# ScalarE and GpSimd in written order while the first half of the values is made

## The chip, the core and the metric

The kernel runs on one core of a Trainium2 chip. The metric is the device time of one execution in microseconds (us). A core has five engines that run at the same time, each with its own list of instructions: TensorE (PE) multiplies matrices into PSUM, VectorE (DVE), ScalarE (ACT) and GpSimd (POOL) work on elements, SyncE (SP) issues most DMA transfers. Each engine works through its list in order; an instruction whose input is not there holds up all that stand behind it on that engine.

## The reference

One inference step of a two-layer decoder on 512 prompt tokens with 16 meta tokens ahead, and on 8 sequences of 4 new tokens: 560 rows of 1024 in all. The first layer is RWKV-7 time mixing, the second latent attention; a squared-ReLU MLP follows each. What matters here is the start of the first layer:

```python
def rwkv7_time_mix(xn, prev, s0, p, i):
    xx = prev - xn
    mu = p['rw_mu'][i]
    xr, xw, xk, xv, xa, xg = (xn + xx * mu[m] for m in range(6))
    r = xr @ p['rw_wr'][i]
    k = xk @ p['rw_wk'][i]
    v = xv @ p['rw_wv'][i]
    w_log = -softplus(-(p['rw_w0'][i] + tanh(xw @ p['rw_w1'][i]) @ p['rw_w2'][i])) - 0.5
    a = sigmoid(p['rw_a0'][i] + (xa @ p['rw_a1'][i]) @ p['rw_a2'][i])
    g = sigmoid(xg @ p['rw_g1'][i]) @ p['rw_g2'][i]
    ...
```

Here xn is the normalised input and prev the row before it. The large products are r, k and v; those with w1, a1 and g1 are narrow (64, 64 and 128 columns) and are called low-rank products here.

## The kernel before, in words

Activations lie feature by feature: eight slices of 128 features (k = 0 to 7), each with the 560 rows as columns. For the values the columns are taken in two spans, 256 and 304. Large products are made three times over, from a rounded high part and a low part (the rest) of each operand: a weight block of 128 x 1024 is loaded by SyncE into one of two buffers `raw`, cast on ScalarE (`whi`), and its low part subtracted on VectorE (`wlo`); the activations are rounded on ScalarE and their low parts subtracted on VectorE in the same way.

`rwkv` makes the first half of the values in one block, `with tc.manual_schedule(engines=MS)` at L537. Within it the engines in the set MS keep the order in which the program is written; all other engines, and all engines outside of it, get their order from a list scheduler, which takes by its own estimate what is ready next. Before, MS holds VectorE alone.

The block first loads two weight blocks (`wload`, casts at L487). Then a loop of 18 steps runs a pipeline over 16 pieces (8 slices for the first span, then 8 for the second). In step n it does, in this written order:

- `s1` of piece n: normalise (L519, VectorE); the difference to the row before (L522, VectorE for some slices, GpSimd for the others); for the first span one column on ScalarE (L524), for the second span the starts of the eight sequences on GpSimd (L526) and a copy for an output on ScalarE (L527);
- in steps 1, 4, 6 and 8 `wlo_`: the low part of the next weight block (L493, VectorE). The first two of these then load and cast the third and the fourth block, which need the buffer that L493 has just read: DMA at L484, cast on ScalarE at L487;
- `s2` of piece n-1: the mix for the values (L447, VectorE) and its rounding `xvh` (L531, ScalarE);
- `s3` of piece n-2: the low part `xvl` (L535, VectorE), and TensorE's products (L503).

Behind the loop the block copies the values of the first span out of PSUM (L514, two on VectorE, two on ScalarE), prefetches the next weight block (cast L307 on ScalarE, low part L308 on VectorE), and makes the low-rank mixes of the eight slices: `lw` on VectorE (L447); two `lm` by `amix`, each a multiplication on ScalarE (L452) and an addition on GpSimd (L453), 15 of them (the last is on VectorE). The copies of the second span stand behind slice 0 of these.

Behind the block follow the low-rank products (L578, L579, L341), the tanh and sigmoid parts, the receptance and key mixes (L447, L459, L460), transposes of the values (`v_out`, L601 to L608), and `stage_a` (L677, L678) and `stage_r` (L326), with which the long part of the layer begins. A product of `stage_r` takes one of the two PSUM buffers that those of L677 hold until ScalarE has read them (L678).

Of the kernel before, what the change touches and what calls it, by code (L numbers as in the profile page):

```python
# [205 lines left out]
class Kern:  # L206
# [203 lines left out]
    def rwkv(self):  # L410
# [64 lines left out]
            nc.scalar.activation(rstd[:, s], q[:, :n], AF.Ln, scale=1.0 / D, bias=self.eps[:, 0:1])  # L475
            nc.scalar.activation(rstd[:, s], rstd[:, s], AF.Exp, scale=-0.5)
        held = lambda n: self.bq_.tile([128, 1024], F32R, tag="b", name=n, bufs=self.nb)
        MS = {mybir.EngineType.DVE}
        raws, wv = [], []

        def wload(*ii):
            for i in ii:
                raw = self.wp.tile([128, 1024], F32, tag="raw", name=f"raw{i}", bufs=2)
                nc.sync.dma_start(raw, self.I["wall"][self.wseq[i]])  # L484
                raws.append(raw)
                hi, lo = held("whi"), held("wlo")
                nc.scalar.copy(hi, raw)  # L487
                wv.append((hi, lo))
            self.wi += len(ii)
# [46 lines left out]

        with tc.manual_schedule(engines=MS):  # L537
            wload(0, 1)
# [1385 lines left out]
```

## Time and profile before

| | |
|---|---|
| median of 3 runs | 1707.78 us (1706.32 to 1708.18) |
| the profiled execution | 1705.09 us |
| its span, first to last instruction | 1703.3 us |
| TensorE busy | 1575.3 us (92%) |
| VectorE busy | 972.1 us (57%) |
| ScalarE busy | 667.0 us (39%) |
| GpSimd busy | 348.4 us (20%) |

The profile is one execution of the kernel, with all times in us from the span's start. A busy share is a mean over stages that are bound by different things. A row of the order in time gives start, duration and the instruction; in square brackets stands how long the engine was idle before it, and for whom it waited. An instruction's duration includes the time in which it has been issued but does not get on.

### The profile page before, as it was taken

The page shows a single profiled execution, that of the slowest core. Times are in us where ns is not written, and L with a number is a line of the kernel's source. Part 1 is how long each engine was busy: PE and PEld are TensorE (multiplying, and loading weights), DVE is VectorE, ACT ScalarE, POOL GpSimd, SP SyncE. Part 2 cuts the span into 40 slices and gives each one's busy share as a digit, 9 for nine tenths or more (in the row PEclk, how much of TensorE's full clock was granted, in tenths as well). Part 3 has the DMA queues.
Part 4 walks back from the last instruction along what each step waited for, and adds up shares of the span by engine and source line. Part 5 has one row for each costly group of instructions (what it writes and reads, how often), then busy time and mean ns, then how long its engine had stood idle before and what let it go on. Part 6 is the DMA issues. An engine that isn't in the chain of part 4 may idle for free.

```text
span 1703.3 us, 33334 instructions
## 1 busy us (share of the span) xinstructions
PE 1575.3 (92%) x13474; PEld 1442.5 (85%) x13474; DVE 972.1 (57%) x1601; ACT 667.0 (39%) x1236; POOL 348.4 (20%) x467
## 2 busy tenths in 40 slices
PE   7699897798899997999999999899999999999996
PEld 6478786686689886999999998767679999999996
DVE  6775678465466677555444656555635444444456
ACT  4374545333445443443331442344534331322222
POOL 3623525442111123000000012773500000000000
PEclk9889897698899998999999999999999999999998
DMA  6334556977834454454232243787612222222223
GB/s 206 128 94 129 181 148 189 256 219 191 241 117 156 158 184 140 137 156 129 87 100 78 86 145 117 230 284 222 190 51 81 91 90 87 88 87 87 87 88 102
DMA packets 156475, 240.04 MB, mean 141 GB/s; under 512 B 68417, under 2 KB 100082, under 8 KB 156322
## 3 DMA queue, kind: packets, MB, share of 16 engines
q1 hardware_dynamic: 140466, 189.59, 36.9%
q0 software_dynamic: 15280, 47.59, 8.5%
q8 instruction: 106, 1.74, 0.4%
q10 hardware_dynamic: 576, 0.74, 0.1%
q14 instruction: 47, 0.39, 0.1%
HBM read 200.50 MB, written 37.37 MB: 140 GB/s over the span
## 4 chain that ended last, share of the span: by engine, by line
PE 54%; DVE 2%; ACT 2%; DMA 1%; issue 1%; SPq 1%; POOL 0%; DVEq 0%; ACTq 0%; POOLq 0%
PE mm L326 31%; PE mm L337 12%; PE sm L337 2%; PE sm L1749 2%; PE sm L1656 1%; PE sm L1700 1%; ACT whi L307 1%; PE sm L1602 1%; DMA lN<-latN,idx 1%; PE sm L1640 0%; DVE wlo L308 0%; PE sm L1703 0%; DMA raw<-wall 0%; DVE y L1861 0%; PE mm L1616 0%
## 5 line engine op out<-in xcount | busy, mean ns | idle before, releaser
L307 ACT CAST whi<-raw 128x1024 fp32r<-128x1024 f32 x218 | 228.8, 1050 | 639.7 <-PE mm L326 356.9
L308 DVE TENSOR_TENSOR wlo<-raw,whi 128x1024 fp32r<-128x1024 f32 x214 | 267.4, 1250 | 280.1 <-ACT whi L307 278.2
L337 PE MATMUL mm<-xs,whi 128*128 128x256 f32 (+1 forms) x1024 | 201.0, 294 | 1.4 <-DVE fd L1316 0.9
L337 PEld LDWEIGHTS mm<-xs,whi 128*128 128x128 f32 x1024 | 163.9, 190 | 2.6 <-issue 1.4
L337 PE MATMUL mm<-xs,wlo 128*128 128x256 f32 (+1 forms) x512 | 149.9, 293 | 0.0
L326 PE MATMUL mm<-hh,wlo 128*128 128x272 f32 (+1 forms) x640 | 133.5, 290 | 0.0
L326 PE MATMUL mm<-hl,whi 128*128 128x272 f32 (+1 forms) x640 | 133.4, 290 | 0.0
L326 PE MATMUL mm<-hh,whi 128*128 128x272 f32 (+1 forms) x640 | 133.3, 290 | 0.0
L326 PE MATMUL mm<-h_ffn,whi 128*128 128x272 f32 x512 | 106.2, 289 | 0.5 <-ACT fr L1350 0.5
L326 PE MATMUL mm<-l_ffn,whi 128*128 128x272 f32 x512 | 105.8, 288 | 0.0
L326 PE MATMUL mm<-h_ffn,wlo 128*128 128x272 f32 x512 | 105.4, 287 | 0.0
L326 PEld LDWEIGHTS mm<-hh,whi 128*128 128x128 f32 x640 | 101.1, 188 | 0.0
L326 PEld LDWEIGHTS mm<-hh,wlo 128*128 128x128 f32 x640 | 100.9, 188 | 0.0
L326 PEld LDWEIGHTS mm<-hl,whi 128*128 128x128 f32 x640 | 100.7, 188 | 0.0
L337 PEld LDWEIGHTS mm<-xs,wlo 128*128 128x128 f32 x512 | 97.1, 190 | 0.1
L1859 POOL TENSOR_TENSOR y<-x,rstd 128x272 f32<-128x272 f32 x4 | 3.5, 895 | 456.6 <-DVE wlo L308 449.7
L337 PE MATMUL mm<-hh,wlo 128*128 128x256 f32 (+1 forms) x256 | 76.2, 298 | 5.0 <-DVE wlo L308 5.0
L326 PEld LDWEIGHTS mm<-h_ffn,whi 128*128 128x128 f32 x512 | 79.9, 188 | 1.0 <-ACT fr L1350 1.0
L326 PEld LDWEIGHTS mm<-l_ffn,whi 128*128 128x128 f32 x512 | 80.2, 188 | 0.0
L326 PEld LDWEIGHTS mm<-h_ffn,wlo 128*128 128x128 f32 x512 | 80.1, 188 | 0.0
L337 PE MATMUL mm<-hl,whi 128*128 128x256 f32 (+1 forms) x256 | 75.8, 296 | 3.0 <-DVE hl L1308 3.0
L337 PE MATMUL mm<-hh,whi 128*128 128x256 f32 (+1 forms) x256 | 76.5, 299 | 0.1
(472 smaller groups left out, 3824.3 us busy)
## 6 DMA issues: line engine op xcount, KB each, us to landing
raw<-wall SPq DMA_DIRECT2D x222, 512.0 KB, 3.6
lT<-latT SPq DMA_DIRECT2D x80, 160.0 KB, 3.6
W_D<-sc POOLq DMA_DIRECT2D x16, 512.0 KB, 3.8
W<-W_D SPq DMA_DIRECT2D x32, 256.0 KB, 4.7
AK_D<-akt SPq DMA_DIRECT2D x8, 576.0 KB, 4.6
s<-state SPq DMA_DIRECT2D x16, 256.0 KB, 3.2
AKc<-AK_D SPq DMA_DIRECT2D x16, 256.0 KB, 4.3
V_D<-vt POOLq DMA_DIRECT2D x8, 288.0 KB, 6.3
```

What stands on the lines that cost most here:

```text
L307: nc.scalar.copy(hi, raw)
L308: self.lo_on.tensor_sub(lo, raw, hi.bitcast(F32))
L326: nc.tensor.matmul(v[:, h, :], wt[:, k, :], xt[:, off + h * n: off + (h + 1) * n], start=(first and k == 0 and e == 0), stop=(last and k = ...
L337: self.nc.tensor.matmul(v, wt[:, k, :], xt, start=(k == 0 and e == 0), stop=(k == len(xs) - 1 and e == 2))
L1602: nc.tensor.matmul(o, l[:, k0:k0 + kw], w[:, 2 + k, :], start=(k == 0 and e == 0), stop=(k == 1 and e == 2))
L1656: nc.tensor.matmul(q[:, q0:], V[h // 2][b][:, 128 * (h % 2):128 * (h % 2) + 128], PT[b] if b else Pm[h % 2], start=(b == 0), stop=(b == 4))
L1700: nc.tensor.matmul(q[32 * bb:32 * bb + 32, cols], qlT[:, r, 4 * g + bb, :], lt[bb][:, :, 128 * r + 64 * k:128 * r + 64 * k + 64], start=(r ...
L1749: nc.tensor.matmul(qa[rs, 0:RANK], PT[jp // 2][:, o:o + 32], nat[bb][:, RANK * k:RANK * k + RANK], start=(jp == 0 and k == 0), stop=False)
L1859: nc.gpsimd.tensor_mul(y[:, i], x[m][:, s], r)
```

## The change

Two engines are added to the set of those that keep the written order in the block. Nothing else is touched: each instruction of the block stays on its engine.

```diff
         held = lambda n: self.bq_.tile([128, 1024], F32R, tag="b", name=n, bufs=self.nb)
-        MS = {mybir.EngineType.DVE}
+        MS = {mybir.EngineType.DVE, mybir.EngineType.Pool, mybir.EngineType.Activation}
         raws, wv = [], []
```

As written, ScalarE's list in the block is: two casts (L487); then step by step L524 or L527, the cast of the third weight block in step 1 and of the fourth in step 4, each ahead of that step's rounding L531; behind the loop two copies L514, the cast L307, two multiplications L452, two copies, and the other 13 multiplications. GpSimd's list is the differences L522 and L526 of all pieces, and behind them the 15 additions L453.

## Rows read from the trace of the kernel before

**Rows 1.** Busy time by stretch: window, length, engines' busy us (instructions), clock, DMA share, GB/s.

```profile
50.00:60.00 10.00, 2.47 (x10) 2.41 (x10) 4.09 (x4) 0.59 (x2) 8.21 (x10) 0.72 0.20 74
100.00:120.00 20.00, 20.00 (x149) 19.49 (x148) 14.17 (x19) 10.70 (x19) 9.41 (x18) 0.95 0.55 151
```

**Rows 2.** Waits from 14 to 70 us: who waited for whom, sum, times, longest.

```profile
DVE mx L447 <- POOL xx L526: 4.7, 1, 4.7
...
DVE xvl L535 <- ACT xvh L531: 3.8, 1, 3.8
```

**Rows 3.** Order in time, GpSimd: start, us, instruction, count, idle before.

```profile
47.69 4.51 POOL L453 TENSOR_TENSOR lm<-lm,xin 128x560 f32<-128x560 f32 x3
...
54.12 0.21 POOL L526 TENSOR_TENSOR xx<-shf,xin 128x8 f32<-128x8 f32 x1
...
60.70 5.64 POOL L453 TENSOR_TENSOR lm<-lm,xin 128x560 f32<-128x560 f32 x4 [2.47 <-ACT lm L452]
...
67.02 3.46 POOL L453 TENSOR_TENSOR lm<-lm,xin 128x560 f32<-128x560 f32 x2
...
72.06 1.37 POOL L453 TENSOR_TENSOR lm<-lm,xin 128x560 f32<-128x560 f32 x1
```

**Rows 4.** Order in time, VectorE.

```profile
21.85 0.42 DVE L535 TENSOR_TENSOR xvl<-mx,xvh 128x256 fp32r<-128x256 f32 x1
...
27.19 0.83 DVE L535 TENSOR_TENSOR xvl<-mx,xvh 128x256 fp32r<-128x256 f32 x1
...
42.00 0.52 DVE L519 SCALAR_TENSOR_TENSOR xin<-xin,vecs,rstd 128x304 f32<-128x304 f32 x1
42.45 0.52 DVE L447 SCALAR_TENSOR_TENSOR mx<-xx,vecs,xin 128x304 f32<-128x304 f32 x1
...
43.77 1.68 DVE L519 SCALAR_TENSOR_TENSOR xin<-xin,vecs,rstd 128x304 f32<-128x304 f32 x1
...
64.39 0.42 DVE L514 COPY V<-mm 128x256 f32<-128x256 f32 x1 [0.64 <-PE mm L503]
...
65.06 2.36 DVE L308 TENSOR_TENSOR wlo<-raw,whi 128x1024 fp32r<-128x1024 f32 x1
67.34 1.90 DVE L447 SCALAR_TENSOR_TENSOR lw<-xx,vecs,xin 128x560 f32<-128x560 f32 x1
...
69.93 7.68 DVE L447 SCALAR_TENSOR_TENSOR lw<-xx,vecs,xin 128x560 f32<-128x560 f32 x7
77.53 0.79 DVE L447 SCALAR_TENSOR_TENSOR lm<-xx,vecs,xin 128x560 f32<-128x560 f32 x1
78.25 1.21 DVE L308 TENSOR_TENSOR wlo<-raw,whi 128x1024 fp32r<-128x1024 f32 x1
...
95.49 2.23 DVE L447 SCALAR_TENSOR_TENSOR mx<-xx,vecs,xin 128x560 f32<-128x560 f32 x3
```

**Rows 5.** Order in time, ScalarE.

```profile
20.72 0.41 ACT L531 CAST xvh<-mx 128x256 fp32r<-128x256 f32 x1
...
23.82 1.05 ACT L487 CAST whi<-raw 128x1024 fp32r<-128x1024 f32 x1 [0.92 <-DMA raw<-wall]
...
29.12 1.05 ACT L487 CAST whi<-raw 128x1024 fp32r<-128x1024 f32 x1 [1.41 <-DMA raw<-wall]
...
59.85 2.72 ACT L452 ACTIVATE lm<-xx,vecs 128x560 f32<-128x560 f32 x4 [3.39 <-PE sm L503]
...
100.75 0.73 ACT L678 ACTIVATE lw<-mm,neg 128x560 f32<-128x560 f32 x1
```

**Rows 6.** Order in time, SyncE's queue: the load of the fourth weight block.

```profile
25.46 0.33 SPq L484 DMA_DIRECT2D raw<-wall  x1
```

**Rows 7.** Order in time, TensorE.

```profile
87.32 1.21 PE L341 MATMUL mm<-lm,l 128*128 128x280 f32 x4
...
91.77 2.90 PE L677 MATMUL mm<-hw,lw 64*128 64x280 f32 x8 [1.74 <-ACT hw L584]
...
102.37 0.50 PE L326 MATMUL mm<-xrh,whi 128*128 128x280 f32 x2
```

## The prediction

> **What bounds the kernel now.** The page came first; its busy shares are means over stages, so I went on to the table of stretches. Between 50 and 60 us TensorE is busy for 2.47 of 10 us and GpSimd for 8.21; between 100 and 120 us TensorE is busy all 20 [rows 1]. So the changed stretch, about 14 to 80 us, isn't paid in TensorE's columns; what counts is when TensorE can start its next long run, the receptance product at 102.37 [rows 7]. I find no slack behind that start, and take its shift for the shift of the end.
>
> Then the waits of the stretch [rows 2], and its engines in order of time [rows 3 to 5]. VectorE already keeps the written order, so one late input stops all of its work. It waits 4.7 us for a small subtraction on GpSimd (L526) of slice 6, which ran only at 54.12, because low-rank additions (L453) had gone first, three of them from 47.69 to 52.20 [rows 2, 3]. It waits 3.8 us for the rounding of slice 7 on ScalarE (L531), ahead of which four low-rank multiplications (L452) were put, from 59.85 to 62.57 [rows 2, 5]. These two waits are what the change removes.
>
> The third thing to see is that VectorE and GpSimd don't run side by side here. The normalising step of a slice takes VectorE 0.52 us at 42.00; the same instruction takes 1.68 at 43.77, while one of GpSimd's additions runs [rows 4]. A weight subtraction takes 2.36 us at 65.06 and 1.21 at 78.25 [rows 4]. GpSimd's additions stretch as well: four from 60.70, while VectorE mostly waits, take 1.41 us each, the two from 67.02 take 1.73 each [rows 3]. One stands while the other goes, and they take turns.
>
> The Trainium skill, "SBUF — State Buffer", section "Who interferes with whom", has this as a rule: a VectorE instruction with two SBUF inputs and a GpSimd instruction that reads SBUF exclude each other, and the later one blocks fully. The rows agree (0.52 against 1.68 us). By it, work that is moved from a place where VectorE stood still anyway to one where it is busy is a loss; if the two could share, the contention term (d) would be nearly gone, and the sum some 11 us of gain.
>
> **The change part by part.** No instruction is added or removed. ScalarE and GpSimd run the block as written.
>
> (a) *Waits on two weight loads, added.* As written, the cast of the third weight block stands ahead of the first rounding (slice 0), and the cast of the fourth ahead of the rounding of slice 3. Before, ScalarE did the rounding of slice 0 at 20.72, and the third cast at 23.82, when its load had landed [rows 5]. Now that rounding waits: cast at 23.82, the next instruction about 0.95 later, its result 0.41 later, so VectorE's low part (L535) starts at 25.2, not at 21.85: +3.35 [rows 4, 5]. Behind it on ScalarE stand all later roundings, and VectorE's whole list waits for them. The fourth load was issued at 25.46, behind the second weight subtraction, and cast at 29.12, 3.66 later [rows 5, 6]. Shifted by 3.35: issued 28.8, cast 32.5, rounding of slice 3 at 33.4, low part at 33.85, not at 27.19 [rows 4]: +6.65 in all.
>
> (b) *Waits on low-rank work, removed.* From the normalising step of slice 6 (43.77) to the first copy of the values (64.39) went 20.6 us. At the undisturbed pace of 1.77 us a slice (42.00 to 43.77) the same list needs two such steps (3.54), one more mix and low part (1.32, from 42.45 to 43.77), a last low part (0.45, a little over the 0.42 of 21.85) and TensorE's last products (0.64, the wait ahead of 64.39): 6.0 us [rows 4]. So the copy comes at 43.77 + 6.65 + 6.0 = 56.4, 8.0 us earlier.
>
> (c) *The next weight block.* Its cast had run inside the block, in an idle moment; it now stands behind two copies on ScalarE, about 0.45 us each by VectorE's like copy (0.42 at 64.39 [rows 4]), and takes 1.05 itself (23.82 [rows 5]). So VectorE's subtraction comes 1.95 us after the first copy instead of 0.67 (64.39 to 65.06 [rows 4]): +1.3. Nothing hides it, since VectorE goes in order.
>
> (d) *Low-rank additions, moved behind the values.* All 15 (eleven had started before 64.39) now run from about 59.0 (copies, cast and one multiplication of 0.68 behind 56.4), against VectorE's eight mixes lw, one lm, two weight subtractions and then the receptance mixes, all with two SBUF inputs. Such an instruction of 560 columns takes 1.90 us when it meets an addition (67.34) and 0.79 when not (77.53): 1.1 each, 16.5 for fifteen. Before, the same list lost 1.15 (65.06), 1.1 (67.34) and, in the seven from 69.93, 7.68 less seven steps of 0.72, 2.6: together 4.9 [rows 4]. Net +11.6. Bounds: if only the ten two-input instructions of the block meet an addition, 11.0 - 4.9 = +6.1; if every addition holds VectorE for its whole 1.41 us [rows 3], 21.2 - 4.9 = +16.3. I take the price of the nearest row.
>
> Sum for VectorE: -8.0 + 1.3 + 11.6 = +4.9 us (bounds -0.6 and +9.6). The last key mix, which ended at 97.7 (95.49 and 2.23 [rows 4]), ends near 102.6.
>
> (e) *What of it reaches 102 us.* One way is by the low-rank products: the additions, at 1.85 us each (between the 1.73 and the 1.90), end at 59.0 + 27.8 = 86.8, not at 73.4 [rows 3]; TensorE's last low-rank product comes about 2 us later, 88.8, against 88.5 (87.32 and 1.21 [rows 7]): +0.3 only, since TensorE had been late with them itself. The other way is by ScalarE: the exponential L678, which frees the PSUM buffer for the receptance product, ran at 100.75 behind the key roundings, and these follow VectorE's mixes; its own input had left TensorE by 94.7 (91.77 and 2.90) [rows 5, 7]. So the start at 102.37 hung on VectorE's list and moves by up to 4.9, by 0.3 on the low-rank path alone. I take 4.2, nearer to VectorE.
>
> (f) GpSimd's small fills and stores behind the block (V's tail, VF_D) move behind 86.8. Those that wait for them, the transposes of the values and what copies them out, ran late already, with the receptance product behind them at 102.37 [rows 7]; so I cost them at nothing. Without that cover they cost up to 86.8 - 73.4 = 13.4 us.
>
> The profiled execution took 1705.09 us, 1.8 more than its span of 1703.3; with +4.2 it would be 1709.3. The median of the runs, 1707.78, is 2.7 above it, so the forecast is 1707.78 + 4.2, near 1712.
>
> **The rivals.** *A, the forecast: VectorE's list carries the delay,* +2 to +9.6, 1710 to 1717. For it: both loads must land before VectorE goes on, and the waits that go away were waits in which GpSimd did work that has to be done anyway. Against: the 11.6 rests on strict turns.
>
> *B, faster: the values' end carries through.* Its place is 56 to 100 us. If the additions cost VectorE little more than before, -8.0 + 1.3 = -6.7 is left: 1701. The point: (d) falls below 6.7 where fewer than about ten instructions meet an addition (10.5 x 1.1 - 4.9 = 6.7). Against it: there are ten in the block alone. For it: transposes and copies out of PSUM, which don't meet GpSimd, could be drawn forward among them.
>
> *C, no change that can be measured:* the start hangs on the low-rank path (+0.3), or on the lower bound of the sum (-0.6): 1707.2 to 1708.1. For it: TensorE was late with these products, by about as much as the additions move.
>
> *D, much slower:* GpSimd's fills and stores behind fifteen additions hold the transposes, and these the PSUM buffers, +13.4: 1721. Against it: their readers come late anyway.
>
> That the change doesn't do what it says has little room: VectorE's 4.7 us wait shows what the written order does to an engine.
>
> **How the numbers follow.** A 0.50, B 0.20, C 0.23, D 0.07. Predicted is A's 1712.0, its own range 1710 to 1717. A fifth of A (0.10) lies within 0.2%, 3.4 us, about what a measurement of this kernel can tell from no change, and all of C: 0.33. The rest of A and D are slower by more, 0.47; B is faster by more, 0.20. The range for 8 in 10 takes in half of B and leaves out D's end: 1702 to 1719.
>
> **What would show it.** (a) ScalarE idle ahead of the third and fourth casts, VectorE idle for about 3 us ahead of two L535. (b) The first value copy near 56 us. (d) Fifteen L453 in one run from about 59 to 87, and mixes lw of about 1.9 us. (e) The receptance product 2 to 5 us behind 102.37. I am wrong if the load waits are absent, if the lw mixes stay near 0.79, or if the receptance product starts before 101.

## The result, and the profile after

The changed kernel takes 1723.59 us (median of 6 runs, 1720.55 to 1727.41), the kernel before 1706.1 beside it: ratio 1.0102, 95% interval 1.0077 to 1.0127. On a second chip it was 1717.34 against 1704.99, ratio 1.0078 (1.0043 to 1.0113). So it is slower, as forecast, but by 12.4 to 17.5 us where 4.2 were predicted; the profiled execution, 1721.25 with a span of 1719.5, is 16.2 longer than that of before.

The changed stretch in order of time, ScalarE first (start, us, instruction, idle before; window 17 to 36 us):

```profile
24.63 1.04 ACT L487 CAST whi<-raw 128x1024 fp32r<-128x1024 f32 x1 [2.54 <-DMA raw<-wall]
25.58 0.40 ACT L531 CAST xvh<-mx 128x256 fp32r<-128x256 f32 x1
...
33.26 1.04 ACT L487 CAST whi<-raw 128x1024 fp32r<-128x1024 f32 x1 [4.60 <-DMA raw<-wall]
```

Both casts stand still for their loads, with the roundings behind them. VectorE pays for it in two waits, 3.13 and 3.20; then the end of the block, and the mixes that follow:

```profile
26.02 0.43 DVE L535 TENSOR_TENSOR xvl<-mx,xvh 128x256 fp32r<-128x256 f32 x1 [3.13 <-ACT xvh L531]
...
34.64 0.43 DVE L535 TENSOR_TENSOR xvl<-mx,xvh 128x256 fp32r<-128x256 f32 x1 [3.20 <-ACT xvh L531]
...
55.12 0.54 DVE L447 SCALAR_TENSOR_TENSOR mx<-xx,vecs,xin 128x304 f32<-128x304 f32 x1 [0.67 <-POOL xx L526]
...
58.44 0.42 DVE L514 COPY V<-mm 128x256 f32<-128x256 f32 x1 [1.80 <-PE mm L503]
...
60.40 1.22 DVE L308 TENSOR_TENSOR wlo<-raw,whi 128x1024 fp32r<-128x1024 f32 x1 [1.20 <-ACT whi L307]
61.54 1.91 DVE L447 SCALAR_TENSOR_TENSOR lw<-xx,vecs,xin 128x560 f32<-128x560 f32 x1
...
76.22 1.91 DVE L447 SCALAR_TENSOR_TENSOR lm<-xx,vecs,xin 128x560 f32<-128x560 f32 x1
...
92.68 0.79 DVE L447 SCALAR_TENSOR_TENSOR mx<-xx,vecs,xin 128x560 f32<-128x560 f32 x1
...
100.92 2.93 DVE L447 SCALAR_TENSOR_TENSOR mx<-xx,vecs,xin 128x560 f32<-128x560 f32 x4
```

The long waits of [rows 2] are gone, the first copy of the values is earlier (58.44, not 64.39 [rows 4]), and the last key mix later (100.92 and 2.93: 103.85, not 97.7). GpSimd shows why: its additions now stand in one run, from 61.10 to 90.78, split only by the issue of four stores.

```profile
61.10 3.58 POOL L453 TENSOR_TENSOR lm<-lm,xin 128x560 f32<-128x560 f32 x2 [5.85 <-ACT lm L452]
64.62 2.17 POOL L615 DMA_DIRECT2D VF_D<-V  x4
66.81 23.97 POOL L453 TENSOR_TENSOR lm<-lm,xin 128x560 f32<-128x560 f32 x13
```

What I had not seen coming is on ScalarE behind the block, and on TensorE after it:

```profile
97.65 1.37 ACT L459 CAST xkh<-mx 128x560 fp32r<-128x560 f32 x2 [0.72 <-DVE mx L447]
99.72 1.37 ACT L459 CAST xkh<-mx 128x560 fp32r<-128x560 f32 x2 [0.71 <-DVE mx L447]
101.80 1.37 ACT L459 CAST xkh<-mx 128x560 fp32r<-128x560 f32 x2 [0.71 <-DVE mx L447]
103.19 1.28 ACT L581 ACT_TABLE_LOAD   x1
104.48 0.63 ACT L581 ACTIVATE hw<-mm 64x560 f32<-64x560 f32 x1
...
106.42 0.62 ACT L584 COPY hw<-mm 64x560 f32<-64x560 f32 x1
...
113.65 0.72 ACT L678 ACTIVATE lw<-mm,neg 128x560 f32<-128x560 f32 x1
```

```profile
91.62 0.64 PE L579 MATMUL mm<-lm,l 128*64 128x280 f32 x2
107.09 2.90 PE L677 MATMUL mm<-hw,lw 64*128 64x280 f32 x8 [14.83 <-ACT hw L584]
...
114.43 0.53 PE L326 MATMUL mm<-xrh,whi 128*128 128x280 f32 x2
```

TensorE ends its low-rank products at 92.26 (91.62 and 0.64). The tanh (L581), which needs only them, stands behind six key roundings in ScalarE's list, each pair waiting 0.7 us for VectorE's key mixes. So the products L677 start at 107.09, not at 91.77, after 14.83 us of idleness, and the receptance product at 114.43, not at 102.37 [rows 7]: +12.06. From there to the first output product (L337), much later, 4 us more are lost. The waits of TensorE between 200 and 420 us differ; first those of before, then those of after (who waited for whom, sum, times, longest):

```profile
PE sm L774 <- DVE AK L749: 12.0, 3, 5.5
PE sm L839 <- DMA xt<-XT_D: 4.2, 1, 4.2
PE sm L847 <- DMA TT<-X_D: 4.1, 2, 3.7
...
PE mm L677 <- ACT r L709: 2.7, 2, 2.4
```

```profile
PE mm L341 <- DVE r L753: 9.6, 2, 7.3
PE sm L774 <- DVE AK L749: 8.0, 2, 4.6
PE mm L677 <- ACT r L709: 5.8, 2, 5.0
PE sm L774 <- POOL av L679: 4.3, 1, 4.3
```

9.6 us of waiting for L753 are new, and two waits for DMA, 8.3 us together, are gone, though no line of that stage was touched: the list scheduler orders it otherwise. With the numbering taken out, the instruction lists of before and after differ on TensorE, VectorE and ScalarE, and most of the differences lie behind the block. The busy times from the receptance product to L337, in the form of [rows 1], before and after:

```profile
102.37:479.90 377.53, 326.02 (x3608) 281.43 (x3605) 237.88 (x472) 173.60 (x384) 138.34 (x221) 0.87 0.66 189
114.43:495.93 381.50, 327.18 (x3606) 282.12 (x3605) 244.30 (x472) 173.71 (x385) 139.90 (x222) 0.87 0.65 188
```

Before, TensorE is busy for 326.0 of 377.5 us and idle for 51.5; after, busy for 327.2 of 381.5 and idle for 54.3. Of the 4.0 us, 2.8 are idle time and 1.2 are longer busy time.

### The profile page after: what moved, and what is told of

It reads as the page before. It is cut to its first block, busy times and chain, and to the rows that moved or that the text cites. A ratio compares the mean times of both kernels' runs of the same rounds, so it can differ in the third digit from the quotient of the medians.

```text
span 1719.5 us, 33333 instructions
## 1 busy us (share of the span) xinstructions
PE 1572.7 (91%) x13474; PEld 1437.6 (84%) x13474; DVE 985.3 (57%) x1601; ACT 667.8 (39%) x1236; POOL 354.9 (21%) x467
## 4 chain that ended last, share of the span: by engine, by line
PE 53%; DVE 2%; DMA 2%; ACT 2%; issue 1%; POOL 0%; DVEq 0%; ACTq 0%; POOLq 0%
PE mm L326 32%; PE mm L337 11%; PE sm L337 2%; PE sm L1749 2%; PE sm L1656 1%; DMA raw<-wall 1%; PE sm L1602 1%; PE sm L1700 1%; DMA lT<-latT,pidx 1%; ACT whi L307 1%; PE sm L1640 1%; DVE wlo L308 1%; DVE y L1861 0%; PE mm L341 0%; PE mm L1616 0%
## 5 line engine op out<-in xcount | busy, mean ns | idle before, releaser
L307 ACT CAST whi<-raw 128x1024 fp32r<-128x1024 f32 x218 | 228.9, 1050 | 643.3 <-PE mm L326 362.9
L337 PE MATMUL mm<-xs,whi 128*128 128x256 f32 (+1 forms) x1024 | 200.1, 293 | 1.4 <-DVE fd L1316 0.9
L337 PEld LDWEIGHTS mm<-xs,whi 128*128 128x128 f32 x1024 | 162.9, 189 | 2.6 <-issue 1.4
L337 PE MATMUL mm<-xs,wlo 128*128 128x256 f32 (+1 forms) x512 | 149.5, 292 | 0.0
L337 PEld LDWEIGHTS mm<-xs,wlo 128*128 128x128 f32 x512 | 96.5, 188 | 0.4 <-DVE wlo L308 0.2
L337 PE MATMUL mm<-hh,wlo 128*128 128x256 f32 (+1 forms) x256 | 76.3, 298 | 5.0 <-DVE wlo L308 5.0
L337 PE MATMUL mm<-hl,whi 128*128 128x256 f32 (+1 forms) x256 | 75.9, 296 | 3.0 <-DVE hl L1308 3.0
L337 PE MATMUL mm<-hh,whi 128*128 128x256 f32 (+1 forms) x256 | 76.6, 299 | 0.5 <-ACT hh L1306 0.3
```

What stands on the lines that cost most here:

```text
L337: self.nc.tensor.matmul(v, wt[:, k, :], xt, start=(k == 0 and e == 0), stop=(k == len(xs) - 1 and e == 2))
```

## The experiments

This table has the readings of every profiled run, in us from the start of its span. The first weight load lands up to 2.5 us apart from run to run, so the receptance product is also given from the first cast (L487 or its new line). The last two columns are its distance to the first product L337 of the output projection, and the shift of that product against before's 479.90.

| kernel | first cast | first value copy | last low-rank product ends | tanh (table load) | last key mix ends | receptance product | from first cast | to L337 | L337 shift | time ratio (95%) |
|---|---|---|---|---|---|---|---|---|---|---|
| before | 17.99 | 64.39 | 88.53 | 87.87 | 97.71 | 102.37 | 84.4 | 377.5 | 0 | 1 |
| after | 18.67 | 58.44 | 92.26 | 103.19 | 103.85 | 114.43 | 95.8 | 381.5 | +16.0 | 1.0102 (1.0077 to 1.0127) |
| after_again | 18.39 | 57.95 | 91.73 | 102.67 | 103.33 | 113.73 | 95.3 | 381.2 | +15.0 | 1.0078 (1.0043 to 1.0113) |
| pool | 16.80 | 51.86 | 84.16 | 84.95 | 93.18 | 99.91 | 83.1 | 378.8 | -1.2 | 0.9989 (0.9971 to 1.0006) |
| casts | 16.13 | 49.81 | 83.59 | 94.52 | 95.18 | 107.44 | 91.3 | 382.3 | +9.8 | 1.0028 (1.0012 to 1.0044) |
| tanh | 16.68 | 56.20 | 89.99 | 94.69 | 101.59 | 109.24 | 92.6 | 383.4 | +12.7 | 1.0060 (1.0039 to 1.0081) |
| casts_tanh | 17.50 | 51.12 | 84.90 | 89.59 | 96.50 | 104.38 | 86.9 | 383.9 | +8.4 | 1.0071 (1.0048 to 1.0094) |
| amix | 18.05 | 57.69 | 81.80 | 80.87 | 99.77 | 101.57 | 83.5 | 380.0 | +1.7 | 1.0023 (1.0007 to 1.0040) |
| casts_amix | 17.29 | 50.97 | 76.04 | 74.92 | 92.83 | 94.63 | 77.3 | 385.7 | +0.4 | 1.0004 (0.9991 to 1.0018) |
| before_amix | 17.89 | 51.31 | 74.12 | 73.10 | 94.10 | 95.48 | 77.6 | 381.2 | -3.2 | 1.0004 (0.9987 to 1.0022) |
| doubled | 17.32 | 56.87 | 116.81 | 119.83 | 119.78 | 131.81 | 114.5 | 382.1 | +34.0 | 1.0192 (1.0149 to 1.0236) |

**pool: GpSimd alone is added to the set.**

```diff
-        MS = {mybir.EngineType.DVE, mybir.EngineType.Pool, mybir.EngineType.Activation}
+        MS = {mybir.EngineType.DVE, mybir.EngineType.Pool}
```

> Written order for VectorE and GpSimd, ScalarE free as before. No cast is held up, no rounding stands behind a late load; the 15 additions still run behind the differences. Theory (ScalarE's written order brings all of the loss): loop as before up to 43 us, first value copy at 51 to 53, additions in one run behind it with lw mixes of 1.9 us, tanh near 86 to 89, receptance product between 99 and 103, time 1700 to 1708. Rival (moving the additions behind the values costs by itself): receptance product at 105 to 108, time 1709 to 1713.

Measured: 1704.69 us against 1704.2, no difference. The receptance product comes 1.3 us earlier than before, from the first cast. GpSimd works off the differences first, as in the changed kernel, but the additions come sooner and overlap the end of the values:

```profile
46.24 9.77 POOL L453 TENSOR_TENSOR lm<-lm,xin 128x560 f32<-128x560 f32 x6
...
56.02 3.65 POOL L453 TENSOR_TENSOR lm<-lm,xin 128x560 f32<-128x560 f32 x2
```

ScalarE, free in its order, gives them their multiplications early. So GpSimd's order as such costs nothing here; the loss comes with ScalarE's. The other half, VectorE and ScalarE without GpSimd, gives instruction by instruction the lists of the changed kernel: once ScalarE keeps its order, GpSimd's additions wait for its multiplications anyway.

**casts: the load waits taken out of ScalarE's list.** The casts of the third and fourth block are written one step later, each behind two roundings that had stood behind it.

```diff
-                hi, lo = held("whi"), held("wlo")
-                nc.scalar.copy(hi, raw)
-                wv.append((hi, lo))
...
+        def wcast(i):
+            wv.append((held("whi"), held("wlo")))
+            nc.scalar.copy(wv[i][0], raws[i])
...
-                    t.append(s2((n - 1) % KT, spans[(n - 1) // KT]))
+                    t.append(s2((n - 1) % KT, spans[(n - 1) // KT])); wcast(n // 2 + 1) if n in (2, 5) else None
```

> The changed kernel with the casts of the third and fourth weight blocks written two steps later (behind the roundings of pieces 1 and 4); their loads are issued where they were. Theory 2 (the two load waits delay the whole list): the loop is 7 us earlier, first value copy at 51 to 52 instead of 58.4, the receptance product near 107.5 instead of 114.4, time about 1717. Rival (what follows is bound by the low-rank additions or by other waits, and takes up the 7 us): receptance product at 112 or later, time 1721 to 1724.

Measured: on ScalarE the waits for the two loads are 1.33 and 1.42 us, and the first rounding no longer stands behind one:

```profile
19.11 0.41 ACT L531 CAST xvh<-mx 128x256 fp32r<-128x256 f32 x1
...
22.10 1.05 ACT L490 CAST whi<-raw 128x1024 fp32r<-128x1024 f32 x1 [1.33 <-DMA raw<-wall]
...
27.52 1.05 ACT L490 CAST whi<-raw 128x1024 fp32r<-128x1024 f32 x1 [1.42 <-DMA raw<-wall]
```

The first value copy comes 33.68 us after the first cast (49.81 - 16.13), not 39.77 as in the changed kernel: 6.1 us, near the 6.65 of term (a). The receptance product gains 4.5 from the first cast, where 7 were expected, and the time falls from 1.0102 to 1.0028, further than expected. Its profiled run is the slowest of its ten (1717.81, median 1711.1), so the +9.8 at L337 is more than the timed runs show. The tanh is as badly placed as before the edit: the products L677 wait 14.8 us for it.

**tanh: the tanh ahead of the key roundings.** They are issued behind `hw` on ScalarE.

```diff
-            nc.scalar.copy(hl[0], t[:, :T])
+            with (tc.issue_after(hwc.ins) if m == 2 else nullcontext()): nc.scalar.copy(hl[0], t[:, :T])
...
-        nc.scalar.copy(hv(hw)[64:128], va[64:128])
+        hwc = nc.scalar.copy(hv(hw)[64:128], va[64:128])
```

> The changed kernel with one edge more: the eight key roundings (L459) stand behind the copy of hw (L584) on ScalarE, so tanh and that copy no longer wait behind six of them. The order up to there is otherwise the changed kernel's. Theory 1 (ScalarE's queue carries the loss): TensorE's low-rank products ended at 92.3 us, so tanh starts near 92.5 and not at 103.2, hw is ready near 96; ScalarE then has the key roundings left, which end with VectorE's last key mix near 104, so the receptance product starts at 106 to 109 instead of 114.4, and the time falls by 5 to 8 us, to about 1717. Rival (VectorE's list alone sets the receptance product): it stays at 113 to 115 and the time stays at 1723.

Measured: the tanh runs 4.7 us after the last low-rank product (94.69 and 89.99) and not 10.9; the receptance product gains 3.2 us from the first cast. It doesn't gain more because the eight key roundings, and what copies out the transposed values, now come behind:

```profile
98.58 2.89 PE L677 MATMUL mm<-hw,lw 64*128 64x280 f32 x8 [8.59 <-ACT hw L584]
103.92 1.54 PE L601 MATMUL sm<-cst,V 128*128 128x128 f32 x6 [2.44 <-ACT vt L606]
...
109.24 0.52 PE L326 MATMUL mm<-xrh,whi 128*128 128x280 f32 x2
```

**casts_tanh: both edits.**

> Both edits: later casts, and key roundings behind hw. If theories 1 and 2 both hold and add up, the receptance product starts near 100 to 101 (114.4 less 7 less 6.5), time 1708 to 1711, within 0.3% of the kernel before. If the receptance product comes at 100 and the time still stands 4 us or more above the kernel before, the rest is lost behind 160 us, in the order that the scheduler gives to later stages (rival).

Measured: the receptance product is 8.9 us nearer to the first cast than in the changed kernel, 2.5 from where it was before. Taking out the load waits and the tanh's place together thus brings back 8.9 of the 11.4 us lost at that point. Both ends were missed: a start of 104.38 for 100 to 101, and 1717.1 us for 1708 to 1711. The time is even 0.4% above that of casts alone, 1.0071 against 1.0028. From the receptance product to L337 this kernel takes 383.9 us, 6.4 more than before (TensorE 3.5 longer idle and 2.9 longer busy). That stage is ordered otherwise once more, but no run separates this order from the busy time. Over all runs the shift at L337, as a share of 1704, lies within the interval of the time ratio, but for casts (0.58%, above it) and before_amix (-0.18%, a little below).

**amix: no addition on GpSimd.** The 15 mixes become whole mixes on VectorE, like the others.

```diff
-    AMIX, LOP = {4: (0, 1, 2, 3, 4, 5, 6, 7), 5: (0, 1, 2, 3, 4, 5, 6)}, {0: (), 2: (7,)}
+    AMIX, LOP = {4: (), 5: ()}, {0: (), 2: (7,)}
```

> The changed kernel with the 15 low-rank additions of GpSimd taken away: each of these 15 mixes (multiplication on ScalarE, addition on GpSimd) becomes one instruction on VectorE, as the other low-rank mixes are. Nothing is left out of the computation. Theory 1 (strict turns: an addition on GpSimd costs VectorE about 1.1 us and takes 1.85 itself, while a whole mix on VectorE alone takes 0.72 to 0.79): VectorE gets 15 x 0.75 = 11 us of new work and loses 15 x 1.1 = 16.5 us of turns, so the last key mix ends about 98 (changed kernel 103.85, before 97.71), the lw mixes take 0.75 us each in place of 1.74 to 1.91, the last low-rank product on TensorE ends near 84 in place of 92.26. Theory 2 (VectorE is simply slow there and GpSimd is not the cause): the last key mix ends at 109 or later and the lw mixes stay above 1.5 us. The load waits on ScalarE stay in both (first low parts as in the changed kernel). If the order of ScalarE behind the block no longer holds the tanh behind six key roundings, the receptance product starts near 102; time 1708 to 1714 by theory 1, 1725 to 1730 by theory 2.

Measured (this run and the next two were on a chip on which the kernel before takes 1750.54 us, so their ratios count, not their times; what that chip adds lies behind L337: from there to the end amix takes 1271.2 us, the kernel before, in its profile from another chip, 1223.4): every mix falls to 0.75 to 0.80 us.

```profile
63.69 0.79 DVE L447 SCALAR_TENSOR_TENSOR lw<-xx,vecs,xin 128x560 f32<-128x560 f32 x1
64.40 1.51 DVE L447 SCALAR_TENSOR_TENSOR lm<-xx,vecs,xin 128x560 f32<-128x560 f32 x2
```

VectorE has 15 instructions more, and its last key mix ends 4.1 us sooner (99.77, expected 98: copies of transposed values, 2.7 us of them, were drawn in between). The tanh, two roundings behind the products, runs at 80.87. The receptance product comes at 101.57, 12.9 before the changed kernel's, and the ratio falls by 0.8%, 13.5 us of 1706. The load waits are all still there (first copy at 57.69). So the additions behind the values, with what queues behind them, are worth more at that point than the load waits. The tanh comes early by this edit too, so the run doesn't separate its place from the additions.

**casts_amix: the additions and the load waits away.** Both diffs together.

> The changed kernel with both of its costs taken away: the casts of the third and fourth weight block are written one s2 later (behind the roundings of slices that do not need them), and the 15 additions of GpSimd are made as whole mixes on VectorE. Nothing is left out. Theory 1 (the loss is the load waits, the turns with GpSimd and the place of the tanh): first value copy near 51, last key mix near 91 (before 97.71), receptance product near 97 (before 102.37), and the time 1697 to 1703, below before's 1704 to 1708. Theory 2 (what decides is the other order of the later stages, between 160 and 480 us, that comes with ScalarE in the set): the receptance product is early as well, but the time stays at or above before, 1704 to 1712.

**before_amix: the kernel before without additions on GpSimd.** The diff of amix on the kernel before, ScalarE and GpSimd free.

> The kernel before with the 15 additions of GpSimd made as whole mixes on VectorE, ScalarE and GpSimd scheduled as before. Nothing is left out. Theory 1 (turns): the 4.7 us wait of VectorE for the small subtraction L526 of slice 6 and the 3.8 us wait for the rounding of slice 7 both go, since no addition and no low-rank multiplication is there to be put ahead; VectorE gets 11 us of mixes; first value copy near 56 in place of 64.39, last key mix near 96 to 99, receptance product at 100 to 102, time 1699 to 1706. Theory 2 (VectorE's work is the limit, GpSimd's additions were free): last key mix at 103 or later, time 1708 to 1714.

Measured: in both the receptance product starts near 95, 7 us earlier than before and earlier than the theory of the turns expected, and in both the time stays where it was, 1.0004, which that theory didn't expect. Casts_amix is 6.2 us ahead of amix from the first cast (77.3 and 83.5), the load waits once more. The time of casts_amix is the one that its second theory gives, but the reason isn't shown. Between the receptance product and L337, casts_amix takes 385.7 us and before_amix 381.2, against 377.5. Of the 8.2 us more in casts_amix only 1.0 are idle time of TensorE (52.5 against 51.5); 7.2 are longer busy time, at a granted clock of 0.85 where before has 0.87:

```profile
94.63:480.32 385.69, 333.20 (x3597) 288.16 (x3597) 241.92 (x470) 172.75 (x382) 137.80 (x222) 0.85 0.63 185
```

That profiled run is also the slowest of its twelve (1757.37, median 1751.29). Before_amix has ScalarE free; TensorE's list is much nearer to that of after than to that of before, and it has the waits of after (200 to 420 us):

```profile
PE sm L774 <- DVE AK L749: 9.7, 2, 5.2
PE mm L341 <- DVE r L753: 9.6, 2, 7.3
PE mm L677 <- ACT r L709: 5.0, 1, 5.0
PE sm L774 <- ACT av L678: 4.3, 1, 4.3
```

So the other order of the later stages doesn't come from ScalarE's written order alone: this edit, too, tips the scheduler into it. Apart from pool (378.8), every variant takes 380 to 386 us there.

**doubled: the additions made twice,** against **after_again**, the changed kernel once more on the same chip.

```diff
-                nc.gpsimd.tensor_add(t, t, xn[k][:, :T])
+                nc.gpsimd.tensor_add(t, t, xn[k][:, :T]); [nc.gpsimd.tensor_add(t, t, xn[k][:, :T]) for _ in range(1) if 2 * k + m - 4 < 16]
```

> The changed kernel with GpSimd's 15 low-rank additions made twice over (each of these mixes has its input added two times; nothing is left out, the order of the later stages stays nearly the changed kernel's). Theory 1 (turns): 30 additions of 1.84 us run from about 61 to 116 us; the some 14 two-input instructions of VectorE that now meet them between 91 and 116 take 1.84 in place of 0.72, +15 us; the last key mix ends near 119 (changed kernel 103.85), the low-rank products near 120 (92.26), the receptance product starts 13 to 17 us later than in the changed kernel, and the time follows it one to one: 13 to 17 us above the changed kernel on the same chip. Theory 2 (the additions are off the path, and the changed kernel's loss is the load waits and the order on ScalarE alone): VectorE's instructions stay at 0.72 to 0.8, the time within 4 us of the changed kernel. Theory 3 (the start at the receptance product has slack behind it): that start moves by 13 to 17 us, the time by less than half.

> The changed kernel once more, on the same chip as the doubled additions, as their baseline: receptance product 11 to 13 us later than in the kernel before, time 0.8 to 1.3 % above before.

Measured: 1736.25 against 1717.34 us, +18.9, a little over the 13 to 17 of theory 1. The lists are those of the changed kernel but for a few places on TensorE and VectorE. GpSimd's additions run to 114.9, and VectorE's mixes take turns with them until then:

```profile
66.11 48.80 POOL L453 TENSOR_TENSOR lm<-lm,xin 128x560 f32<-128x560 f32 x27
```

```profile
102.66 3.73 DVE L447 SCALAR_TENSOR_TENSOR mx<-xx,vecs,xin 128x560 f32<-128x560 f32 x2
106.31 3.73 DVE L460 TENSOR_TENSOR xrl<-mx,xrh 128x560 fp32r<-128x560 f32 x2
...
113.61 6.18 DVE L447 SCALAR_TENSOR_TENSOR mx<-xx,vecs,xin 128x560 f32<-128x560 f32 x7
```

Between 102.66 and 110 each takes 1.83 us, 0.72 to 0.79 in the changed kernel at the same place; of the seven from 113.61 only the first meets an addition. The last key mix ends 16.45 us later than in after_again, the receptance product starts 18.08 later, L337 19.0, and the span is 18.5 longer. With the later order all but kept, the shift of that start is the shift of the end.

## Why the prediction was wrong, step by step

**(a) was right.** Low part of slice 3 predicted at 33.85, measured at 34.64, against 27.19: +7.45 for the +6.65; 0.68 of the rest is this run's later first load (18.67 and 17.99). The waits that were to show it are there, 2.54 and 4.60 on ScalarE, 3.13 and 3.20 on VectorE.

**(b) was right in kind, 2.0 us too large.** The copy came at 58.44 for 56.4. The low part of slice 3 brought 0.8 of it. At the end TensorE set the pace: VectorE waited 1.80 for it, where I had put the 0.64 of [rows 4], and 0.67 for a subtraction L526 that stood behind GpSimd's issue of a store; the loop between was 0.6 shorter than I had counted.

**(c) was right:** 1.96 us from the copy to the weight subtraction (58.44 to 60.40), predicted 1.95.

**(d) was right.** From the first copy to the last key mix went 45.4 us, 33.3 before: +12.1, of which (c) is 1.3, so 10.8 for the predicted 11.6. The lw mixes took 1.91 us where they met additions, and each addition 1.84 (23.97 by 13). The rule of the Trainium skill ("SBUF — State Buffer", "Who interferes with whom"), that a VectorE instruction with two SBUF inputs and a GpSimd instruction reading SBUF exclude each other, agrees with this: 1.83 in turns in doubled, 0.75 to 0.80 without additions in amix. VectorE's sum is -5.95 + 1.3 + 10.8 = +6.1, predicted +4.9, within its bounds.

**(e) is the step that failed,** in three ways, and the path that it names was misread as well: before, TensorE's transposes ran right up to the receptance product, while L678 had freed the buffer at 101.48 [rows 5], 0.9 us sooner:

```profile
100.80 1.82 PE L601 MATMUL sm<-cst,V 128*128 128x128 f32 x9
```

I let VectorE's +4.9 arrive as 4.2; it arrived whole, 6.1. I took ScalarE's order behind the block for the old one: before, the tanh ran at 87.87, beside VectorE's mixes; after, behind six key roundings, so that table loads, tanh, L584 and L677 (103.19 to 109.99) came behind VectorE's list and not beside it. That is the other 5.9 of the +12.06. The runs show 3.2 to 4.4 of it as due to the tanh's place (tanh against after, casts_tanh against casts, from the first cast); the rest of the 5.9, the order of the transposes and of L678, wasn't tried by itself. And "its shift for the shift of the end", from the prediction's first part, holds, 18.08 to 18.5 in doubled, only while the later stages keep their order. They didn't, and another 4.0 were lost up to L337, 2.8 of them idle time of TensorE and 1.2 longer busy time. That the other order cost them is argued from the waits; no run takes it back by itself. Sum: 4.2 predicted, +1.9, +5.9 and +4.0 make 16.0, where the span grew by 16.2.

**(f) shows no cost, but not for the reason given.** The fills and stores don't stand behind the additions: the stores VF_D were issued at 64.62, among them. The set fixes the order of the block's own instructions; others are still let in between.

Of the rivals, B's gain at the first copy was real and was eaten by (d), as argued against it; C and D didn't happen, though the time is past D's 1721: its price came by another way. What the range lacked was a bound on (e) from ScalarE's queue: a tanh held up to the end of VectorE's list, with the 3.85 us from its table load to the end of L584 and the 2.90 of L677 behind it.

What stays open: how much of the loss behind the receptance product is the other order and how much is slower TensorE, which decision of the scheduler tips the order of the later stages, and whether an order like that of before could be had with the earlier start of before_amix. None of the kernels run here is measurably faster than the kernel before.

## What to carry to other kernels

Writing one engine's order by hand moves the waits that the scheduler had kept off it into that order: look at what each instruction in the new list waits for, a load above all, and then at what the scheduler puts behind the block on the same engine, since a short step on the critical path can land behind a queue that waits for another engine. Before moving GpSimd work from an idle place to a busy one of VectorE, count the two-input instructions it will meet and charge each the full turn. And where a scheduler orders the rest, expect any edit to reorder far-off stages. The stretch behind the receptance product was 1 to 8 us longer in the variants here, part of it longer busy time of TensorE: compare instruction lists, and busy with idle time, before crediting or blaming the edit.

## What the runs showed of the hardware

VectorE and GpSimd don't always take turns one for one. In pool one lw mix stood for 10.27 us while GpSimd made seven additions, 1.34 us each, with a few fills between them. When the stores came in their place, the next three mixes took 0.79 or less each:

```profile
60.19 10.27 DVE L447 SCALAR_TENSOR_TENSOR lw<-xx,vecs,xin 128x560 f32<-128x560 f32 x1
70.38 2.21 DVE L447 SCALAR_TENSOR_TENSOR lw<-xx,vecs,xin 128x560 f32<-128x560 f32 x3
```

```profile
60.40 4.04 POOL L453 TENSOR_TENSOR lm<-lm,xin 128x560 f32<-128x560 f32 x3
...
64.52 5.34 POOL L453 TENSOR_TENSOR lm<-lm,xin 128x560 f32<-128x560 f32 x4
69.81 2.18 POOL L615 DMA_DIRECT2D VF_D<-V  x4
```

Beside stores with additions right before and behind them mixes were slow too (two took 2.98 us together from 64.14 in the changed kernel); what held those isn't shown. In pool the issue of stores alone doesn't hold VectorE; additions do, and a mix can lose to several in a row. An addition costs VectorE about 1.1 us in turns (1.91 less 0.79), and its whole 1.34 where GpSimd goes on without a turn. What decides between the two isn't shown.
